# One-hot gate products of an expert layer: two 12-bit products in place of one fp32 product, and three of four plain masks made on ScalarE

## The chip, the cores and the metric

The kernel runs on one core of a Trainium2 chip. The metric is the time of one execution on the device in microseconds (us). Engines are named as the profile names them: PE is the matrix engine (PEld its loads of stationary operands), DVE the vector engine, ACT the scalar engine, POOL GpSimd, SP the queue that issues most transfers.

## The reference

The reference is a stack of three transformer layers on 256 tokens of width 1024. The change lies in the last part of the last layer, a layer of 16384 single-neuron experts of which every token uses 8 heads x 16:

```python
def peer(h, w_q, sub_keys, u_tab, v_tab):
    ...
    top_s, pos = lax.top_k(cand_s, PEER_TOPK)
    experts = jnp.take_along_axis(cand_i, pos, axis=-1)
    gates = jax.nn.softmax(top_s, axis=-1).astype(h.dtype)
    ...
    def one_chunk(args):
        hc, ec, gc = args
        u = u_tab[ec]
        a = jax.nn.gelu(jnp.einsum('td,thkd->thk', hc, u), approximate=False)
        return jnp.einsum('thk,thkd->td', gc * a, v_tab[ec])
```

An expert's number is 128 e + r with e (the block) and r (the row) from 0 to 127. `top_k` gives each token 128 (expert, gate) pairs.

## The kernel before, in words

The kernel does not gather experts. It computes gelu(h u) for all 16384 experts and all 256 tokens, multiplies it by a table W of gates that is zero where a token does not use an expert, and multiplies the result by all of v. This is `Peer.run`. Its first loop runs over b = 0..127, the blocks of 128 experts, in an order that is written out by hand: inside it ACT, DVE, POOL and PE each execute in the order in which the code names their instructions.

In one pass of that loop, `stream(b + 2)` loads a 512 KB block of u and splits it in a rounded part (`uhi`, ACT, L1235) and a rest (`ulo`, L1236, on POOL once the gates have begun); `first(b)` issues 24 products of 128x128 by 128x256 (L117 to L119); and `gelu` takes two finished blocks through ACT into W (L1258, L1261), with `times` (DVE, L1267) multiplying in the gates that are already there. `work` makes the gates' indices in between: DVE's top-16 searches up to about block 51, then `softmax` and `turn`, which lays experts' e, r and gates out by token in `col`.

From there on the gate table is built, five tokens with each pass (`RATE`). `masks_of` makes two 128x128 masks for a token on DVE: `a` (L1200) holds the gate where the place number equals e, `b` (L1201) holds one where it equals r. Both read the place numbers 0..127 from `places`, a copy of `iota` in a PSUM bank. `gates_of` multiplies them on PE (L1210) in fp32, which the trace records as two instructions for each product, and sums so the token's 128x128 gate table. `gates_out`, once for four tokens, copies the table's blocks that have no gelu yet to W on ACT (L1221) and multiplies the others into W on DVE (L1223). The masks lie in eight buffers in turn, and PE takes them four tokens late (`HOT`, `LAG`). The second loop, which multiplies W by v, is not touched.

Of the kernel before, what the change touches and what calls it, by code (L numbers as in the profile page):

```python
# [9 lines left out]
F32 = mybir.dt.float32  # L10
F32R = mybir.dt.float32r
# [3 lines left out]
AF = mybir.ActivationFunctionType  # L15
OP = mybir.AluOpType
# [6 lines left out]
S = 256  # L23
NT = 2
# [7 lines left out]
NCAND = sum((b - a) * w for a, b, w in RECT)  # L32
# [3 lines left out]
LEAD = 2  # L36
EARLY = 45
SPARE = 1.6
RATE = 5
HOT, LAG = 8, 4  # L40
PE = mybir.EngineType.PE
ORDERED = (mybir.EngineType.Activation, mybir.EngineType.DVE, mybir.EngineType.Pool, PE)
KEYS = ((1, 0), (0, 1), (2, 0), (3, 0), (1, 1), (2, 1), (3, 1))
# [40 lines left out]
class Net:  # L84
    def __init__(self, tc, ins, out, dbg):
        self.tc, self.nc, self.i, self.out, self.dbg = tc, tc.nc, ins, out, dbg
        self.bg = []
        self.n, self.pace, self.credit = 0, 1.2, 0.0
        self.normed = None
        self.mod, self.gate, self.loose = {}, {}, set()  # L90
# [1032 lines left out]
class Peer:  # L1123
# [3 lines left out]
    def __init__(self, net, s, pools):  # L1127
        self.net, self.s = net, s
        self.sp = sp = pools("route", 2)
        self.ef = [sp.tile([128, 128], F32, name=f"ef{t}", bufs=1) for t in range(NT)]  # L1130
        self.v = [sp.tile([128, 8, 16], F32, name=f"v{t}", bufs=1) for t in range(NT)]
        self.iota = sp.tile([128, 128], F32, name="iota", bufs=1)
        net.nc.gpsimd.dma_start(self.iota, net.i["k_iota"])
        self.line, self.full, self.count = [], [], 0
        self.parts = {}
        self.gated = self.active = 0

    def route(self, t, h):

        net, sp, s = self.net, self.sp, self.s  # L1140
        nc = net.nc
        one = sp.tile([128, 2, 16], F32, name="one")
        two = sp.tile([128, 2, 16], F32, name="two")
        both = sp.tile([128, 2, NCAND], F32, name="both")
        cs, ci = both[:, 0, :], both[:, 1, :]
        yield from top16(net, sp, s[t][:, 2 * h, :], 128, "t1", one[:, 0, :], one[:, 1, :], 128.0)
        yield from top16(net, sp, s[t][:, 2 * h + 1, :], 128, "t2", two[:, 0, :], two[:, 1, :], None)
        o = 0
        for a, b, wd in RECT:
            n = (b - a) * wd  # L1150
            nc.vector.tensor_tensor(both[:, :, o:o + n].rearrange("p m (a b) -> p m a b", b=wd),
                                    one[:, :, a:b, None].to_broadcast([128, 2, b - a, wd]),
                                    two[:, :, None, :wd].to_broadcast([128, 2, b - a, wd]), op=OP.add)
            o += n
        yield 0.8
        pos = sp.tile([128, 16], F32, name="pos")
        yield from top16(net, sp, cs, NCAND, "t3", self.v[t][:, h, :], pos, None)
        j = sp.tile([128, 16, NCAND], F32, name="ej", bufs=1)
        for k in range(16):
            nc.vector.scalar_tensor_tensor(j[:, k, :], self.iota[:, :NCAND], pos[:, k:k + 1], ci, op0=OP.is_equal,  # L1160
                                           op1=OP.mult, accum_out=self.ef[t][:, h * 16 + k:h * 16 + k + 1])
            if k % 4 == 3:
                yield 0.8
# [13 lines left out]
    def turn(self, t):  # L1177

        net, sp = self.net, self.sp
        nc = net.nc  # L1180
        x = sp.tile([128, 864], F32, name="ej", bufs=1)[:, :512].rearrange("p (a b) -> p a b", a=4)
        i0, i1 = x[:, 2, :].bitcast(I32), x[:, 3, :].bitcast(I32)
        nc.vector.tensor_copy(i0, self.ef[t])
        nc.vector.tensor_scalar(i1, i0, 7, None, op0=OP.arith_shift_right)
        nc.vector.tensor_copy(x[:, 0, :], i1)
        nc.vector.scalar_tensor_tensor(x[:, 1, :], x[:, 0, :], -128.0, self.ef[t], op0=OP.mult, op1=OP.add)
        p = net.wk()
        for k in range(2):
            nc.tensor.transpose(p[:, k * 128:(k + 1) * 128], x[:, k, :], net.ident)
        nc.tensor.transpose(p[:, 256:384], self.v[t].rearrange("p a b -> p (a b)"), net.ident)  # L1190
        nc.scalar.activation(self.col[:, t], p[:, :384].rearrange("p (k t) -> p k t", k=3), AF.Copy)

    def masks_of(self, n):

        nc = self.net.nc
        t, m = divmod(n, 128)
        a, b = (self.masks[:, self.count % HOT, j, :] for j in range(2))
        self.count += 1
        col = self.col[:, t]
        nc.vector.tensor_scalar(a, self.places, col[:, 0, m:m + 1], col[:, 2, m:m + 1], op0=OP.is_equal, op1=OP.mult)  # L1200
        nc.vector.tensor_scalar(b, self.places, col[:, 1, m:m + 1], None, op0=OP.is_equal)  # L1201
        self.line.append((n, a, b))

    def gates_of(self):

        n, a, b = self.line.pop(0)
        if n % 4 == 0:
            self.p = self.net.wk()
        k = n % 4
        self.net.nc.tensor.matmul(self.p[:, k * 128:(k + 1) * 128], b, a, start=True, stop=True)  # L1210
        if k == 3:
            self.full.append((n - 3, self.p))

    def gates_out(self):

# [67 lines left out]
    def run(self, W, h2T, spill):  # L1283

        net = self.net
        nc = net.nc
        self.W, self.h2T = W, h2T
        self.outs, self.late = [], []

        def work():  # L1290

            for n in range(1, 16):
                yield from self.route(n // 8, n % 8)
            cols = net.x8([128, 2048])
            self.col = cols[:, 0:768].rearrange("p (t k n) -> p t k n", t=NT, k=3)
            self.masks = net.x8([128, HOT, 2, 128])
            self.places = net.acc()[:, :128]
            nc.vector.tensor_copy(self.places, self.iota)
            self.tmp = [net.wk().rearrange("p (e t) -> p e t", e=2) for _ in range(2)]
            for t in range(NT):  # L1300
                self.softmax(t)
                yield 1.5
            for t in range(NT):
                self.turn(t)
                yield 1.0

        bg, credit, todo = work(), EARLY, list(range(S))
        for b in range(128):
            if b:
                credit += SPARE  # L1310
            while bg and credit > 0:
                cost = next(bg, None)
                if cost is None:
                    bg = None
                else:
                    credit -= cost
            if b + LEAD < 256:
                self.stream(b + LEAD, not bg and b + LEAD < 128)
            self.first(b)
            if not bg and todo is not None:  # L1320
                for _ in range(RATE):
                    if todo:
                        self.masks_of(todo.pop(0))
                    if len(self.line) > LAG or not todo:
                        if self.line:
                            self.gates_of()
                    if self.full:
                        self.gates_out()
                if not todo:
                    while self.line:  # L1330
                        self.gates_of()
                        if self.full:
                            self.gates_out()
                    todo = None
            self.times()
            if len(self.outs) > 1 or b == 127:
                while self.outs:
                    self.gelu()
                    if b < 127:
                        break  # L1340
        assert todo is None
        self.times()
        self.acc = {(t, c): net.acc() for t in range(NT) for c in range(2)}
        self.wx = net.x8([128, 4, 2, S], F32R)
        for e in range(2):
            self.weights(e)
        net.X = net.xp.tile([128, NT, D], F32, name="X")
        nc.gpsimd.dma_start(net.X, spill.rearrange("(t p) d -> p t d", p=128))
        for e in range(128):
            if e + LEAD < 128:  # L1350
                self.stream(128 + e + LEAD)
            if e + 2 < 128:
                self.weights(e + 2)
            self.second(e)
        for t in range(NT):
            for c in range(2):
                x = net.X[:, t, c * 512:(c + 1) * 512]
                nc.vector.tensor_tensor(x, x, self.acc[t, c], op=OP.add)
                (nc.scalar if c else nc.sync).dma_start(net.out[0, t * 128:(t + 1) * 128, c * 512:(c + 1) * 512], x)
# [259 lines left out]
```

## Time and profile before

| | us |
|---|---|
| median of three runs | 1845.95 (1845.42 to 1848.73) |
| the profiled execution | 1847.4, of which its span is 1845.6 |
| first loop, before the gate masks (1040.7 to 1195.3) | 154.6 |
| first loop, with gate masks (1195.3 to 1413.8) | 218.5 |
| first loop, after them (1413.8 to 1481.5) | 67.7 |

The span is the time from the first to the last instruction of the profiled execution; 1.8 us of that execution lie around it. The stages are stretches of the span, in us from its start. A single matrix product's duration includes the way through the array, so the pace of PE is read from the distance of starts or from counts over a stretch, not from durations.

### The profile page before, as it was taken

What the parts mean: (1) busy time and instruction counts of PE and PEld (TensorE: products, weight loads), DVE (VectorE), ACT (ScalarE), POOL (GpSimd) and SP (SyncE); (2) the same over time, 40 slices, a digit from 0 to 9 for tenths busy, and PEclk for the clock granted to TensorE, in tenths of its full rate; (3) what the DMA queues carried; (4) which work ended last, traced back from release to release, by engine and by line L of the source; (5) the groups of instructions that cost most, each with busy time, mean ns of one, the idle gap of its engine ahead of it and who ended that gap; (6) DMA issues with size and microseconds to landing.
All of it is one profiled execution on the core that took longest, in us unless ns stands there. A gap on an engine that the chain in (4) does not pass through costs nothing.

```text
span 1845.6 us, 28886 instructions
## 1 busy us (share of the span) xinstructions
PE 1772.3 (96%) x10804; PEld 1502.0 (81%) x10804; DVE 1296.4 (70%) x3228; ACT 862.5 (47%) x1258; POOL 218.9 (12%) x165
## 2 busy tenths in 40 slices
PE   7998999998999998998999999999999999999999
PEld 4764789887979997776885699999999978888887
DVE  3676788767876547785568899889997155555554
ACT  2444555544455435465543344544444444444443
POOL 2000000000000000000000000055556800000000
PEclk9999999998999999997999999999999999999999
DMA  9865379976757643553664166544444666666664
GB/s 356 253 209 170 115 247 317 311 254 216 260 173 253 195 150 115 182 169 96 193 233 144 60 185 184 168 130 125 135 118 143 186 207 191 185 190 186 189 187 149
DMA packets 144444, 347.38 MB, mean 188 GB/s; under 512 B 12469, under 2 KB 29901, under 8 KB 143152
## 3 DMA queue, kind: packets, MB, share of 16 engines
q1 hardware_dynamic: 139040, 331.93, 56.5%
q0 software_dynamic: 4688, 12.03, 2.0%
q8 instruction: 85, 1.39, 0.3%
q10 hardware_dynamic: 576, 1.57, 0.2%
q14 instruction: 55, 0.45, 0.1%
HBM read 343.36 MB, written 3.70 MB: 188 GB/s over the span
## 4 chain that ended last, share of the span: by engine, by line
PE 78%; DVE 15%; DMA 3%; ACT 3%; issue 1%; SPq 0%; DVEq 0%; ACTq 0%
PE acc L117 19%; PE acc L119 19%; PE acc L118 18%; PE wk L117 4%; PE wk L119 4%; PE wk L118 4%; DVE x L1200 2%; DVE ulo L1236 2%; PE wk L1210 2%; DVE x L1201 2%; PE acc L1072 2%; DVE W L1223 1%; DVE ej L1160 1%; DMA adaw<-in_ada_w 1%; PE wk L537 1%
## 5 line engine op out<-in xcount | busy, mean ns | idle before, releaser
L134 DVE TENSOR_TENSOR wlo<-raw,whi 128x1024 fp32r<-128x1024 f32 (+1 forms) x260 | 312.8, 1214 | 145.8 <-ACT whi L133 144.7
L1235 ACT ACTIVATE uhi<-raw 128x1024 fp32r<-128x1024 f32 x256 | 271.6, 1061 | 293.3 <-PE acc L119 177.8
L133 ACT ACTIVATE whi<-raw 128x1024 fp32r<-128x1024 f32 (+1 forms) x260 | 271.6, 1053 | 276.6 <-PE acc L119 96.7
L1236 DVE TENSOR_TENSOR ulo<-raw,uhi 128x1024 fp32r<-128x1024 f32 x182 | 222.5, 1223 | 174.3 <-ACT uhi L1235 173.9
L117 PE MATMUL acc<-x,uhi 128*128 128x256 f32 x1024 | 293.4, 287 | 0.0
L118 PE MATMUL acc<-X,uhi 128*128 128x256 f32 x1024 | 288.4, 282 | 0.0
L119 PE MATMUL acc<-x,ulo 128*128 128x256 f32 x1024 | 288.2, 281 | 0.0
L117 PE MATMUL acc<-whi,hT 128*128 128x512 f32 (+1 forms) x528 | 210.6, 400 | 9.4 <-ACT hT L138 7.6
L1236 POOL TENSOR_TENSOR ulo<-raw,uhi 128x1024 fp32r<-128x1024 f32 x74 | 177.0, 2393 | 352.5 <-ACT uhi L1235 352.4
L118 PE MATMUL acc<-wlo,hT 128*128 128x512 f32 (+1 forms) x528 | 207.3, 393 | 0.8 <-DVE wlo L134 0.7
L119 PE MATMUL acc<-whi,hT 128*128 128x512 f32 (+1 forms) x528 | 207.4, 393 | 0.3
L117 PE MATMUL acc<-uhi,x 128*128 128x512 f32 x512 | 202.3, 395 | 1.0 <-ACT x L138 1.0
L119 PE MATMUL acc<-uhi,x 128*128 128x512 f32 x512 | 202.3, 395 | 0.0
L118 PE MATMUL acc<-ulo,x 128*128 128x512 f32 x512 | 202.2, 395 | 0.0
L117 PEld LDWEIGHTS acc<-x,uhi 128*128 128x128 f32 x1024 | 193.9, 189 | 0.2 <-issue 0.2
L118 PEld LDWEIGHTS acc<-X,uhi 128*128 128x128 f32 x1024 | 193.8, 189 | 0.2 <-issue 0.2
L119 PEld LDWEIGHTS acc<-x,ulo 128*128 128x128 f32 x1024 | 193.7, 189 | 0.0
L117 PE MATMUL wk<-hT,whi 128*128 128x256 f32 x608 | 172.4, 284 | 0.0
L118 PE MATMUL wk<-hT,whi 128*128 128x256 f32 x608 | 171.9, 283 | 0.0
L119 PE MATMUL wk<-hT,wlo 128*128 128x256 f32 x608 | 171.8, 283 | 0.0
L117 PEld LDWEIGHTS acc<-whi,hT 128*128 128x128 f32 x528 | 101.1, 192 | 36.9 <-ACT hT L138 10.9
L119 PEld LDWEIGHTS acc<-whi,hT 128*128 128x128 f32 x528 | 101.0, 191 | 24.6 <-DVE hT L139 2.6
(371 smaller groups left out, 3057.4 us busy)
## 6 DMA issues: line engine op xcount, KB each, us to landing
raw<-in_mlp_w SPq DMA_DIRECT2D x128, 512.0 KB, 5.0
raw<-in_k_ut SPq DMA_DIRECT2D x128, 512.0 KB, 3.6
raw<-in_peer_v SPq DMA_DIRECT2D x128, 512.0 KB, 4.0
adaw<-in_ada_w SPq DMA_DIRECT2D x80, 512.0 KB, 5.0
raw<-in_w_in SPq DMA_DIRECT2D x52, 512.0 KB, 4.0
raw<-in_conv_w_in SPq DMA_DIRECT2D x24, 512.0 KB, 5.3
a<-in_k_a SPq DMA_DIRECT2D x8, 1024.0 KB, 8.2
raw<-in_attn_w_in SPq DMA_DIRECT2D x16, 512.0 KB, 8.2
```

The source lines that it names most:

```text
L117: nc.tensor.matmul(ps, ak(a[0]), bk(b[0]), start=start, stop=False, skip_group_check=True)
L118: nc.tensor.matmul(ps, ak(a[0]), bk(b[1]), start=False, stop=False, skip_group_check=True)
L119: self.last = nc.tensor.matmul(ps, ak(a[1]), bk(b[0]), start=False, stop=stop, skip_group_check=True)
L133: self.high = nc.scalar.activation(hi[:, :, :w], raw[:, :, :w], AF.Copy)
L134: self.low = nc.vector.tensor_tensor(lo[:, :, :w], raw[:, :, :w], hi[:, :, :w].bitcast(F32), op=OP.subtract)
L537: nc.tensor.transpose(p[:, k * 128:(k + 1) * 128], src[:, k * 128:(k + 1) * 128], net.ident)
L1072: nc.tensor.matmul(ps, self.hT[:, k, t * 128:(t + 1) * 128], self.slabs[c][k // 2][:, k % 2, j * n * 128:(j + 1) * n * 128], start=(k == 0 ...
L1200: nc.vector.tensor_scalar(a, self.places, col[:, 0, m:m + 1], col[:, 2, m:m + 1], op0=OP.is_equal, op1=OP.mult)
L1201: nc.vector.tensor_scalar(b, self.places, col[:, 1, m:m + 1], None, op0=OP.is_equal)
L1210: self.net.nc.tensor.matmul(self.p[:, k * 128:(k + 1) * 128], b, a, start=True, stop=True)
L1235: nc.scalar.activation(hi, raw, AF.Copy)
L1236: (nc.gpsimd if aside else nc.vector).tensor_tensor(lo, raw, hi.bitcast(F32), op=OP.subtract)
```

## The change

Each gate is cut in two parts that the reduced-precision type float32r (as which `uhi`, `ulo` and the activations already go to PE) holds exactly: a rounded gate (`col` row 3) and the rest (row 4). For each token DVE makes two `a` masks, one for each part, and PE sums two products, each one float32r product of 128x128 by 128x128. The plain masks `b` of three tokens of four are made on ACT: Square of (place - r), then one Relu(1 - square) over the three. The fourth `b` stays on DVE. `masks_of` and `gates_of` now take a group of four tokens, one group with each pass of the loop; the masks of a group lie in one of two halves of a buffer, and PE takes them one pass later. A pass first names the products of the group before, then the masks of its group, then `gates_out` of the group before.

```diff
-        self.col = cols[:, 0:768].rearrange("p (t k n) -> p t k n", t=NT, k=3)
-        self.masks = net.x8([128, HOT, 2, 128])
+        self.col = cols[:, 0:1536].rearrange("p (t k n) -> p t k n", t=NT, k=6)
+        self.one = cols[:, 1536:1537]
...
-        nc.scalar.activation(self.col[:, t], p[:, :384].rearrange("p (k t) -> p k t", k=3), AF.Copy)
+        col = self.col[:, t]
+        nc.scalar.activation(col[:, 0:3], p[:, :384].rearrange("p (k t) -> p k t", k=3), AF.Copy)
+        nc.scalar.activation(col[:, 3].bitcast(F32R), p[:, 256:384], AF.Copy)
+        nc.scalar.activation(col[:, 5], p[:, 128:256], AF.Copy, scale=-1.0)
+        nc.vector.tensor_tensor(col[:, 4], col[:, 2], col[:, 3], op=OP.subtract)
...
     def masks_of(self, n):
-        t, m = divmod(n, 128)
-        a, b = (self.masks[:, self.count % HOT, j, :] for j in range(2))
...
-        nc.vector.tensor_scalar(a, self.places, col[:, 0, m:m + 1], col[:, 2, m:m + 1], op0=OP.is_equal, op1=OP.mult)
-        nc.vector.tensor_scalar(b, self.places, col[:, 1, m:m + 1], None, op0=OP.is_equal)
+        t, g = n // 128, n // 4 % 2
+        a, b, col = self.hot[0][:, g], self.hot[1][:, g], self.col[:, t]
+        for k in range(4):
+            m = (n + k) % 128
+            for j in range(2):
+                nc.vector.tensor_scalar(a[:, k, j, :], self.places, col[:, 0, m:m + 1], col[:, 3 + j, m:m + 1],
+                                        op0=OP.is_equal, op1=OP.mult)
+            if k < 3:
+                nc.scalar.activation(b[:, k, :], self.places, AF.Square, bias=col[:, 5, m:m + 1])
+            else:
+                nc.vector.tensor_scalar(b[:, k, :], self.places, col[:, 1, m:m + 1], None, op0=OP.is_equal)
+        nc.scalar.activation(b[:, 0:3, :], b[:, 0:3, :].bitcast(F32), AF.Relu, scale=-1.0, bias=self.one)
         self.line.append((n, a, b))
...
-        self.net.nc.tensor.matmul(self.p[:, k * 128:(k + 1) * 128], b, a, start=True, stop=True)
+        for k in range(4):
+            for j in range(2):
+                self.net.nc.tensor.matmul(p[:, k * 128:(k + 1) * 128], b[:, k, :], a[:, k, j, :], start=(j == 0),
+                                          stop=(j == 1), skip_group_check=True)
...
-        bg, credit, todo = work(), EARLY, list(range(S))
+        bg, credit, todo = work(), EARLY, list(range(0, S, 4))
...
-                for _ in range(RATE):
-                    if todo:
-                        self.masks_of(todo.pop(0))
-                    if len(self.line) > LAG or not todo:
-                        if self.line:
-                            self.gates_of()
-                    if self.full:
-                        self.gates_out()
...
+                if self.line:
+                    self.gates_of()
+                if todo:
+                    self.masks_of(todo.pop(0))
+                if self.full:
+                    self.gates_out()
```

How the instructions stand on DVE before, early in the gate stage, between two of the multiplications into W (L1223); `acc` is the bank of `places`, the two `x` are the mask buffers and `col`; a wait in brackets names the engine whose counter is waited for:

```order
L1223 TENSOR_TENSOR W<-wk,W 128x4x52 [waits Activation_49]
L1200 TENSOR_SCALAR x_11836<-acc,x_11835 128x128 [waits DVE_49]
L1201 TENSOR_SCALAR x_11836<-acc,x_11835 128x128 [waits DVE_49]
L1200 TENSOR_SCALAR x_11836<-acc,x_11835 128x128 [waits DVE_49]
L1201 TENSOR_SCALAR x_11836<-acc,x_11835 128x128 [waits DVE_49]
```

And the same place of the changed kernel, between two of its multiplications (there L1232; L1203 is an `a` mask, L1209 the `b` mask that stays):

```order
L1232 TENSOR_TENSOR W<-wk,W 128x4x52 [waits Activation_49]
L1203 TENSOR_SCALAR x_11974<-acc,x_11835 128x128 [waits DVE_49] x2
L1203 TENSOR_SCALAR x_11974<-acc,x_11835 128x128 [waits Activation_49]
L1203 TENSOR_SCALAR x_11974<-acc,x_11835 128x128 [waits DVE_49]
L1203 TENSOR_SCALAR x_11974<-acc,x_11835 128x128 [waits Activation_49]
L1203 TENSOR_SCALAR x_11974<-acc,x_11835 128x128 [waits DVE_49]
L1203 TENSOR_SCALAR x_11974<-acc,x_11835 128x128 [waits Activation_49]
L1203 TENSOR_SCALAR x_11974<-acc,x_11835 128x128 [waits DVE_49]
L1209 TENSOR_SCALAR ej<-acc,x_11835 128x128 [waits DVE_49]
L1232 TENSOR_TENSOR W<-wk,W 128x4x54 [waits Activation_49]
L1276 TENSOR_TENSOR W<-W,wk 128x2x12
```

Before, no mask waits for ACT; now the first `a` mask of the second, third and fourth token does. By the counts of the program, each of these three waits is for the Square of the token just before it.

ACT before, in the same stretch, from one split of u (L1235) to the next:

```order
L1235 ACTIVATE uhi<-raw 128x1024 [waits DMAHW3_49,Pool_49]
L1221 ACTIVATE W<-wk 128x4x76 [waits PE_49] x2
L1258 ACTIVATE wk<-acc 128x2x16 [waits DVE_49]
L1261 ACTIVATE W<-acc 128x2x240
L1235 ACTIVATE uhi<-raw 128x1024 [waits DMAHW4_49,Pool_49]
```

ACT now (L1244 is the split of u, L1207 Square, L1210 Relu, L1230 the copy to W, L1267 and L1270 gelu):

```order
L1210 ACTIVATE ej<-ej,x_11835 128x384 [waits Activation_49]
L1230 ACTIVATE W<-wk 128x4x76 [waits PE_49]
L1267 ACTIVATE wk<-acc 128x2x12
L1270 ACTIVATE W<-acc 128x2x244
L1244 ACTIVATE uhi<-raw 128x1024 [waits DMAHW4_49,Pool_49]
L1207 ACTIVATE ej<-acc,x_11835 128x128 [waits DVE_49] x3
L1210 ACTIVATE ej<-ej,x_11835 128x384 [waits Activation_49]
L1230 ACTIVATE W<-wk 128x4x74 [waits PE_49]
```

Four more instructions stand between a split and the copy to W, and each Square waits for DVE: by the counts, for the second `a` mask of its own token. No table load stands between Square, Relu and Gelu. On PE, where five fp32 products stood behind a block's 24, eight products of the new kind stand now:

```order
L117 MATMUL acc<-x_9392,ulo 128x256
L1219 MATMUL wk<-x_11974,ej 128x128 [waits DVE_49,PE_49,Activation_49]
L1219 MATMUL wk<-x_11974,ej 128x128 [waits DVE_49] x6
L1219 MATMUL wk<-x_11974,ej 128x128
L115 MATMUL acc<-x_9392,uhi 128x256
```

The first of them waits for the Relu of its group, and the later ones for the group's DVE masks.

## Rows read from the trace of the kernel before

**Rows 1.** Busy time by engine, with gate masks and after: us, engines, PEclk, DMA share, GB/s.

```profile
1195.30:1413.80 218.50, 212.06 (x1779) 208.65 (x1779) 206.77 (x603) 97.09 (x169) 124.24 (x52) 1.00 0.42 127
1413.80:1481.50 67.70, 67.34 (x570) 67.14 (x568) 11.85 (x16) 31.59 (x38) 52.95 (x23) 1.00 0.60 184
```

**Rows 2.** The same stretches, L117 alone, eight instructions a block: PE, PEld.

```profile
1195.30:1413.80 218.50, 122.78 (x421) 79.47 (x422) 1.00 0.42 127
1413.80:1481.50 67.70, 53.12 (x190) 35.58 (x189) 1.00 0.60 184
```

**Rows 3.** Groups of instructions of the gate stage: xcount | busy us, mean ns | idle before.

```profile
L1200 DVE TENSOR_SCALAR x<-acc,x 128x128 f32<-128x128 f32 x256 | 105.6, 412 | 0.0
L1201 DVE TENSOR_SCALAR x<-acc,x 128x128 f32<-128x128 f32 x256 | 89.9, 351 | 0.0
L1210 PE MATMUL wk<-x 128*128 128x128 f32 x512 | 70.6, 278 | 6.4 <-DVE x L1201 3.5 <-ACT W L1221 2.7
L1223 DVE TENSOR_TENSOR W<-wk,W 128x224 f32<-128x224 f32 (+25 forms) x64 | 55.3, 863 | 11.7 <-ACT W L1221 11.2
L1221 ACT ACTIVATE W<-wk 128x288 f32<-128x288 f32 (+25 forms) x64 | 34.6, 541 | 118.8 <-PE wk L1210 118.8
L1267 DVE TENSOR_TENSOR W<-W,wk 128x512 f32<-128x512 f32 (+25 forms) x39 | 20.0, 512 | 47.8 <-ACT wk L1258 47.8
```

**Rows 4.** Timeline of DVE in the gate stage: start us, us, what.

```profile
1339.98 0.96 DVE L1223 TENSOR_TENSOR W<-wk,W 128x336 f32<-128x336 f32 x1
1340.84 0.40 DVE L1200 TENSOR_SCALAR x<-acc,x 128x128 f32<-128x128 f32 x1
1341.16 0.34 DVE L1201 TENSOR_SCALAR x<-acc,x 128x128 f32<-128x128 f32 x1
1341.42 0.40 DVE L1200 TENSOR_SCALAR x<-acc,x 128x128 f32<-128x128 f32 x1
```

**Rows 5.** Timeline of ACT in the gate stage, a gelu and the split behind it.

```profile
1344.49 0.56 ACT L1258 ACTIVATE wk<-acc 128x352 f32<-128x352 f32 x1
...
1345.16 1.06 ACT L1235 ACTIVATE uhi<-raw 128x1024 fp32r<-128x1024 f32 x1
```

**Rows 6.** Line 202 (min/median/max ns), and timelines of a transpose's read-out, ACT and DVE.

```profile
L202 ACT ACTIVATE hT<-wk,vec x8: 360/368/368, 958.9 to 985.9; 128x128 f32<-128x128 f32 x8
...
422.10 0.41 DVE L207 TENSOR_SCALAR full<-wk,af1A,af1B 128x128 f32<-128x128 f32 x1 [1.08 <-PE wk L193]
...
423.34 0.96 DVE L207 TENSOR_SCALAR full<-wk,af1A,af1B 128x128 f32<-128x128 f32 x2
...
422.55 0.46 ACT L202 ACTIVATE full<-wk,af1B,af1A 128x128 f32<-128x128 f32 x1 [0.29 <-DVE full L207]
423.40 0.46 ACT L202 ACTIVATE full<-wk,af1B,af1A 128x128 f32<-128x128 f32 x1 [0.40 <-DVE full L207]
```

**Rows 7.** Timeline of ACT in `turn`: 384 elements, and the next instruction.

```profile
1196.80 0.49 ACT L1191 ACTIVATE x<-wk 128x384 f32<-128x384 f32 x1 [1.36 <-PE wk L1190]
1197.19 1.05 ACT L1235 ACTIVATE uhi<-raw 128x1024 fp32r<-128x1024 f32 x1
```

**Rows 8.** Timelines of PE with idle before in brackets, windows of 1 us (PEclk third last).

```profile
167.63 0.66 PE L395 MATMUL wk<-ident,adab 128*128 128x128 f32 x4 [1.75 <-DVE adab L380]
...
168.00:169.00 1.00, 1.00 (x5) 0.36 (x5) 0.95 (x4) 0.00 (x0) 0.82 (x2) 0.72 0.68 275
...
974.80 0.44 PE L537 MATMUL wk<-ident,mr 128*128 128x128 f32 x2 [2.06 <-ACT mr L1076]
...
976.00:977.00 1.00, 1.00 (x7) 0.90 (x7) 0.90 (x8) 0.20 (x2) 0.00 (x0) 1.00 0.28 25
...
1193.38 0.41 PE L117 MATMUL acc<-x,uhi 128*128 128x256 f32 x1
1193.60 0.41 PE L118 MATMUL acc<-X,uhi 128*128 128x256 f32 x1
...
1195.91 0.29 PE L117 MATMUL acc<-x,uhi 128*128 128x256 f32 x1
```

More of the change, by code (lines that the diff above doesn't have):

```diff
@@ L38 @@
 SPARE = 1.6
-RATE = 5
-HOT, LAG = 8, 4
 PE = mybir.EngineType.PE
@@ L1133, in __init__ @@
         net.nc.gpsimd.dma_start(self.iota, net.i["k_iota"])
-        self.line, self.full, self.count = [], [], 0
+        self.line, self.full = [], []
         self.parts = {}
@@ L1157, in route @@
         yield from top16(net, sp, cs, NCAND, "t3", self.v[t][:, h, :], pos, None)
-        j = sp.tile([128, 16, NCAND], F32, name="ej", bufs=1)
+        j = sp.tile([128, 1024], F32, name="ej", bufs=1)[:, :16 * NCAND].rearrange("p (k n) -> p k n", k=16)
         for k in range(16):
@@ L1180, in turn @@
         nc = net.nc
-        x = sp.tile([128, 864], F32, name="ej", bufs=1)[:, :512].rearrange("p (a b) -> p a b", a=4)
+        x = sp.tile([128, 1024], F32, name="ej", bufs=1)[:, :512].rearrange("p (a b) -> p a b", a=4)
         i0, i1 = x[:, 2, :].bitcast(I32), x[:, 3, :].bitcast(I32)
@@ L1190, in turn @@
         nc.tensor.transpose(p[:, 256:384], self.v[t].rearrange("p a b -> p (a b)"), net.ident)
-        nc.scalar.activation(self.col[:, t], p[:, :384].rearrange("p (k t) -> p k t", k=3), AF.Copy)
+        col = self.col[:, t]
[3 more added lines that the diff above has]
+        nc.vector.tensor_tensor(col[:, 4], col[:, 2], col[:, 3], op=OP.subtract)
     def masks_of(self, n):
         nc = self.net.nc
-        t, m = divmod(n, 128)
-        a, b = (self.masks[:, self.count % HOT, j, :] for j in range(2))
-        self.count += 1
-        col = self.col[:, t]
-        nc.vector.tensor_scalar(a, self.places, col[:, 0, m:m + 1], col[:, 2, m:m + 1], op0=OP.is_equal, op1=OP.mult)
-        nc.vector.tensor_scalar(b, self.places, col[:, 1, m:m + 1], None, op0=OP.is_equal)
+        t, g = n // 128, n // 4 % 2
[10 more added lines that the diff above has]
+        nc.scalar.activation(b[:, 0:3, :], b[:, 0:3, :].bitcast(F32), AF.Relu, scale=-1.0, bias=self.one)
         self.line.append((n, a, b))
@@ L1206, in gates_of @@
         n, a, b = self.line.pop(0)
-        if n % 4 == 0:
-            self.p = self.net.wk()
-        k = n % 4
-        self.net.nc.tensor.matmul(self.p[:, k * 128:(k + 1) * 128], b, a, start=True, stop=True)
-        if k == 3:
-            self.full.append((n - 3, self.p))
+        p = self.net.wk()
+        for k in range(4):
+            for j in range(2):
+                self.net.nc.tensor.matmul(p[:, k * 128:(k + 1) * 128], b[:, k, :], a[:, k, j, :], start=(j == 0),
+                                          stop=(j == 1), skip_group_check=True)
+        self.full.append((n, p))
     def gates_out(self):
@@ L1294, in work @@
             cols = net.x8([128, 2048])
-            self.col = cols[:, 0:768].rearrange("p (t k n) -> p t k n", t=NT, k=3)
-            self.masks = net.x8([128, HOT, 2, 128])
+            self.col = cols[:, 0:1536].rearrange("p (t k n) -> p t k n", t=NT, k=6)
+            self.one = cols[:, 1536:1537]
+            nc.vector.memset(self.one, 1.0)
             self.places = net.acc()[:, :128]
@@ L1305, in work @@
                 yield 1.0
-        bg, credit, todo = work(), EARLY, list(range(S))
+            self.hot = (net.x8([128, 2, 4, 2, 128], F32R),
+                        self.sp.tile([128, 1024], F32R, name="ej", bufs=1).rearrange("p (g k n) -> p g k n", g=2, k=4))
+        bg, credit, todo = work(), EARLY, list(range(0, S, 4))
         for b in range(128):
@@ L1320, in run @@
             if not bg and todo is not None:
-                for _ in range(RATE):
-                    if todo:
-                        self.masks_of(todo.pop(0))
-                    if len(self.line) > LAG or not todo:
-                        if self.line:
-                            self.gates_of()
-                    if self.full:
-                        self.gates_out()
[L1329 to L1333, printed above, removed]
+                if self.line:
[4 more added lines that the diff above has]
+                    self.gates_out()
+                if not todo and not self.line:
                     todo = None
```

## The prediction

> **What bounds the kernel now.** I read the busy times by stretch first. While the gate table is built, DVE is busy 206.8 and PE 212.1 of 218.5 us; behind it PE is busy 67.3 of 67.7 [rows 1]. The reader is to see two engines at their limit side by side in the gate stage, and PE alone after it. Second, the same stretches for L117 alone, which stands eight times in a block [rows 2]: 421 instructions are 52.6 blocks with gates, 190 are 23.75 blocks without. So a block costs 67.7 / 23.75 = 2.85 us where PE sets the pace, and the gate stage 218.5 - 52.6 x 2.85 = 68.6 us more than its blocks alone. This 68.6 us is all that the change can win or must pay for. Third, the groups by line [rows 3] and DVE's timeline [rows 4]: a mask with a gate (L1200) holds DVE for 0.32 us from its start to the next one's, a plain mask (L1201) for 0.26; the multiplication into W (L1223, mean 0.86) is left 0.10 before it ends, so it holds DVE for 0.76. Fourth, the waits in the groups: DVE idles 0.0 before the masks, so before the change nothing stands between one mask and the next.
>
> **The change, part by part.**
>
> PE loses 512 recorded fp32 instructions. PE's busy time less the blocks is 212.1 - 149.9 = 62.2 us, 0.12 each. It gains eight float32r products of 128 columns for each group of four tokens. The trace has none. Below: half of a 256-column one, whose pace is 2.85 / 24 = 0.119, so 0.06. Above: as much as an fp32 product, 0.24. PE's block then takes 2.85 + 0.48 to 2.85 + 1.92, 3.3 to 4.8 us; I take the lower end, since one instruction passes where two did. It does not enter the sum if a block takes longer than 4.8 for other reasons, which is the case below.
>
> DVE's work for a group is eight `a` masks at 0.32, one `b` at 0.26, one multiplication into W at 0.76, and every second block the gelu's multiplication (mean 0.51, less the same 0.10, halved: 0.21): 3.79 us if nothing interrupts it. For 64 groups that is 64 x (3.79 - 2.85) = 60 us above the blocks, against 68.6 before. By busy time alone the change would win 8 us: for four tokens it adds four gate masks, at 0.32, and drops four plain ones but for one, at 0.26.
>
> But the masks are interrupted. The order of the changed kernel has DVE wait, at the second, third and fourth token, for ACT's Square of the token before, and each Square wait for DVE's two masks of its own token. Both read `places` in one PSUM bank. The trace of before shows the same pattern in the read-out of transposes, where DVE and ACT take turns on one bank [rows 6]: DVE ends at 422.10 + 0.41 = 422.51 and ACT starts at 422.55; ACT, started at 423.40, ends at 423.86, and the second DVE instruction of the pair from 423.34, 0.41 long, starts at 423.89. They never overlap on a bank; a handover costs 0.04 one way, 0.03 the other. The Trainium skill, page "PSUM — Partial Sum Buffer", section "PSUM bank collisions raise a hardware error", says that two engines must not access one bank in the same 32 partitions at once, reads against reads included, and that software has to keep them apart by bank; it speaks against placing ACT's masks here. By that rule the chain below is the sum, and by the view of busy times alone it would be the 8 us gain; the trace agrees with the rule.
>
> So I add up the chain of one block, from one copy to W on ACT to the next:
> - the copy, 0.54 (L1221's mean, [rows 3]), handover 0.03, DVE's multiplication 0.76, half a gelu multiplication 0.21, the first pair of masks 0.32 + 0.41 to its end = 0.73, handover 0.04: 2.31. ACT's own way in a block with gelu is 0.44 for the copy, 0.67 from a gelu to the split behind it, 0.96 for the split [rows 5], together 2.07: not later.
> - three Squares. The nearest row is an ACT instruction on 128x128 from PSUM with one pointer operand, 0.37 [rows 6]: 1.11. Between them two returns with a pair of masks, 0.03 + 0.73 + 0.04 each: 1.60.
> - then the Relu and the next copy, in order on ACT. 384 elements hold ACT 0.39 us [rows 7]; the pointer operand adds 0.46 - 0.37 = 0.09 [rows 6], its wait for the last Square 0.03: 0.51. DVE's last three masks take 0.03 + 0.32 + 0.32 + 0.34 = 1.01 in the same time, and the copy ends 0.51 + 0.54 behind the Square: they are hidden.
>
> Together 2.31 + 2.71 + 0.51 = 5.53 us for four tokens, above PE's 3.3 to 4.8. The 64 groups cost 64 x (5.53 - 2.85) = 171.5 us above the blocks in place of 68.6: **+103 us**. `turn` gains two ACT copies of 0.37 and a DVE subtraction of about 0.35 for each half of the tokens, ahead of the first masks: 0 to 2.2 us, I take 1. The sum is +104 us: 1847.4 + 104 = 1951.4 for a profiled execution, and 1846 + 104 = 1950 for the median, which lies 1.4 us below that execution.
>
> What is hidden and stays hidden: the split on POOL and the transfers, since blocks become longer; PE's products, unless they take over 2.7 us a block. What is late next is PE: it waits for masks 0.7 to 2.2 us in every block.
>
> Bounds. A pair of masks could end after 0.66 (0.32 + 0.34, as a plain mask does) or 0.82 (no overlap); a Square could take 0.46 like an instruction with two pointers; the Relu might pay no pointer; the six handovers might cost nothing, 0.2. A block then takes 5.03 to 6.07 us, the change costs 71 to 138, and the time lies at 1917 to 1984.
>
> **The rivals.**
> 1. *DVE alone sets the pace (faster).* If ACT's Squares cost DVE nothing, a block takes 3.79 us: 60 - 68.6 = -8 us, 1838. For it: busy times; the order of L1200 shows that DVE never waits today. Against it: the waits named in the order, which must be passed three times in a block. It decides if a block takes under 2.85 + 68.6 / 64 = 3.92 us. That needs the three Squares with their handovers, 1.3 us, and ACT's Relu and copy to vanish. Chance 0.04, and 0.01 that it lands within 0.2% of no change, which is about what a measurement can tell.
> 2. *PE falls to its lower clock.* With pauses of 0.7 to 2.2 us in every block PE may lose clock. A pause of 1.75 us at 167 was followed by a mean granted clock of 0.72, one of 2.06 at 975 by 1.00 [rows 8], so rows are of two minds. At 1.2 GHz products start 0.22 apart (1193.38, 1193.60), 24 take 5.3 us, and eight gate products twice 0.48 or more: 6.2 us a block or above, 64 x 3.35 - 68.6 = +146, 1992 and up. Against it: at that clock PE has no pauses left, and after 1193 the distance of durations was back at the fast level (0.29 at 1195.91). PE may also come late before ACT's copy feels it: the group's last mask ends some 0.5 us behind the copy's start, the products take up to 1.9, and the next copy is 5.5 away, which leaves 3 us. Chance that it holds for most of the stage: 0.09.
> 3. The forecast, waits between DVE and ACT with PE off the path: 0.86.
>
> **How the numbers follow.** The forecast is 1950. Its bounds give 1917 to 1984; I cut a little below, where three bounds must meet, and reach above into the second rival for clock falls in part of the stage: 1920 to 1990. Left out are most of rival 2, rival 1 and the forecast's edges, together just under 0.2. Faster by over 0.2%: 0.04; within: 0.01; slower: 0.95.
>
> **What the profile afterwards will show.** Right: DVE's masks idle for ACT's Square, three times a block, 0.4 us or more each; the Square idles for DVE's mask; splits of u start about 5.5 us apart in the stage, which lasts some 355 us for 64 blocks; PE's gate products wait for the last mask or the Relu; 11 blocks are left behind it in place of 24. Wrong: masks of DVE that start 0.32 apart across tokens (rival 1); products of u 0.22 apart through the stage (rival 2); a Square or Relu far from 0.37 and 0.5, which would change the size, not the sign.

## The result, and the profile after

The changed kernel takes 1953.19 us (median of four runs, 1950.52 to 1956.27) against 1845.68 us before (1845.17 to 1848.73): the ratio is 1.0579, with a 95% interval of 1.056 to 1.0599. The profiled execution took 1950.52 us, 103.1 us more than the one of before (1847.4).

The busy times and the granted clock on the page of the changed kernel (40 equal slices, in tenths):

```profile
PE   7998999989999989989999998788887899999999
...
DVE  3667787778775567855698997777777635555555
...
PEclk9999999989999999979999999988888899999999
```

The gate stage is about slices 25 to 32: there PE falls to seven or eight tenths and DVE to six or seven, where before they stood side by side near their limit [rows 1]. The stage by itself and the blocks left behind it (busy time of PE, PEld, DVE, ACT and POOL, granted clock, share of the DMA engines, GB/s):

```profile
1202.80:1549.00 346.20, 277.48 (x2025) 267.12 (x2024) 258.45 (x661) 206.17 (x443) 150.31 (x63) 0.92 0.32 98
1549.00:1582.00 33.00, 33.00 (x264) 33.00 (x264) 8.21 (x11) 15.38 (x19) 23.88 (x10) 0.95 0.55 166
```

The groups that answer to [rows 3] (L1203 is an `a` mask, L1207 the Square, L1210 the Relu, L1230 the copy to W, L1232 the multiplication into W, L1219 a gate product), over the gate stage:

```profile
L1203 DVE TENSOR_SCALAR x<-acc,x 128x128 fp32r<-128x128 f32 x509 | 185.2, 405 | 83.7 <-ACT ej L1207 83.7
...
L1219 PE MATMUL wk<-x,ej 128*128 128x128 f32 x512 | 72.3, 285 | 68.7 <-ACT ej L1210 68.5
L1207 ACT ACTIVATE ej<-acc,x 128x128 fp32r<-128x128 f32 x191 | 70.2, 367 | 139.6 <-DVE x L1203 138.9
...
L1232 DVE TENSOR_TENSOR W<-wk,W 128x200 f32<-128x200 f32 (+31 forms) x64 | 58.5, 914 | 5.3 <-ACT W L1230 3.9
L1210 ACT ACTIVATE ej<-ej,x 128x384 fp32r<-128x384 f32 x64 | 39.4, 615 | 2.1
L1230 ACT ACTIVATE W<-wk 128x312 f32<-128x312 f32 (+31 forms) x64 | 30.3, 473 | 0.0
```

The idle column is what to read. Before, it was 0.0 ahead of every mask; now DVE's masks stand 83.7 us for ACT's Square and the Squares stand 138.9 us for DVE's masks. The two wait for each other, and none of the 576 masks on DVE overlaps any of the 192 Squares in time. The chain of one block (start, length, what held it):

```profile
1402.09 0.94 DVE W L1232
1403.02 0.65 DVE x L1203 x2
1403.67 0.03 issue
1403.70 0.38 ACT ej L1207
1404.07 0.03 issue
1404.10 0.74 DVE x L1203 x2
1404.84 0.02 issue
...
1406.03 0.38 ACT ej L1207
1406.40 0.03 issue
1406.43 0.73 DVE x L1203 x2
1407.16 0.26 DVE ej L1209
...
1407.42 0.97 DVE W L1232
```

ACT's timeline behind the last of these Squares, Relu and copy to W:

```profile
1406.43 0.62 ACT L1210 ACTIVATE ej<-ej,x 128x384 fp32r<-128x384 f32 x1
1406.95 0.44 ACT L1230 ACTIVATE W<-wk 128x160 f32<-128x160 f32 x1
```

The copy reads the PSUM tile `wk` while DVE's last masks (1406.43 to 1407.42) read the bank of `places`, and neither waits for the other. So it is the one bank that is taken in turns, and not PSUM as such.

From 1402.09 to 1407.42 is 5.33 us for one group of four tokens. DVE's timeline gives the next group, which has a gelu multiplication, 1407.42 to 1413.15 = 5.73 (idle before an instruction, and what ended it, in brackets):

```profile
1407.42 0.97 DVE L1232 TENSOR_TENSOR W<-wk,W 128x352 f32<-128x352 f32 x1
1408.30 0.46 DVE L1276 TENSOR_TENSOR W<-W,wk 128x296 f32<-128x296 f32 x1
...
1409.84 0.73 DVE L1203 TENSOR_SCALAR x<-acc,x 128x128 fp32r<-128x128 f32 x2 [0.44 <-ACT ej L1207]
1411.01 0.73 DVE L1203 TENSOR_SCALAR x<-acc,x 128x128 fp32r<-128x128 f32 x2 [0.44 <-ACT ej L1207]
1412.17 0.73 DVE L1203 TENSOR_SCALAR x<-acc,x 128x128 fp32r<-128x128 f32 x2 [0.44 <-ACT ej L1207]
...
1413.15 0.97 DVE L1232 TENSOR_TENSOR W<-wk,W 128x352 f32<-128x352 f32 x1
```

Three waits of 0.44 us stand in each group; the mean of the two groups is 5.53 us.

### The profile page after: what moved, and what is told of

The parts are those of the page before. It is cut to its first block, busy times and chain, and to the rows that moved or that the text cites. A ratio compares the mean times of both kernels' runs of the same rounds, so it can differ in the third digit from the quotient of the medians.

```text
span 1948.7 us, 29223 instructions
## 1 busy us (share of the span) xinstructions
PE 1810.6 (93%) x10804; PEld 1533.3 (79%) x10804; DVE 1350.0 (69%) x3295; ACT 960.2 (49%) x1525; POOL 219.7 (11%) x165
## 4 chain that ended last, share of the span: by engine, by line
PE 68%; DVE 18%; ACT 8%; DMA 3%; issue 2%; SPq 0%; DVEq 0%; ACTq 0%
PE acc L115 17%; PE acc L117 17%; PE acc L116 16%; DVE x L1203 7%; PE wk L115 4%; PE wk L117 4%; PE wk L116 4%; ACT ej L1207 4%; DVE W L1232 2%; PE acc L1070 1%; ACT uhi L1244 1%; ACT W L1230 1%; DVE wlo L132 1%; DMA adaw<-in_ada_w 1%; PE wk L535 1%
## 5 line engine op out<-in xcount | busy, mean ns | idle before, releaser
L1244 ACT ACTIVATE uhi<-raw 128x1024 fp32r<-128x1024 f32 x256 | 271.2, 1060 | 277.7 <-PE acc L117 179.2
L115 PE MATMUL acc<-x,uhi 128*128 128x256 f32 x1024 | 305.1, 298 | 0.0
L117 PE MATMUL acc<-x,ulo 128*128 128x256 f32 x1024 | 300.7, 294 | 0.0
L116 PE MATMUL acc<-X,uhi 128*128 128x256 f32 x1024 | 299.5, 292 | 0.0
L1203 DVE TENSOR_SCALAR x<-acc,x 128x128 fp32r<-128x128 f32 x512 | 186.2, 405 | 84.2 <-ACT ej L1207 84.2
L117 PE MATMUL acc<-whi,hT 128*128 128x512 f32 (+1 forms) x528 | 207.0, 392 | 0.3
L116 PEld LDWEIGHTS acc<-X,uhi 128*128 128x128 f32 x1024 | 206.7, 202 | 0.2 <-issue 0.2
L115 PEld LDWEIGHTS acc<-x,uhi 128*128 128x128 f32 x1024 | 206.0, 201 | 0.2 <-issue 0.2
L117 PEld LDWEIGHTS acc<-x,ulo 128*128 128x128 f32 x1024 | 204.5, 200 | 0.0
L117 PE MATMUL acc<-uhi,x 128*128 128x512 f32 x512 | 203.1, 397 | 0.0
L117 PE MATMUL wk<-hT,wlo 128*128 128x256 f32 x608 | 171.8, 283 | 0.0
L1207 ACT ACTIVATE ej<-acc,x 128x128 fp32r<-128x128 f32 x192 | 70.5, 367 | 139.6 <-DVE x L1203 138.9
```

What stands on the lines that cost most here:

```text
L115: nc.tensor.matmul(ps, ak(a[0]), bk(b[0]), start=start, stop=False, skip_group_check=True)
L116: nc.tensor.matmul(ps, ak(a[0]), bk(b[1]), start=False, stop=False, skip_group_check=True)
L117: self.last = nc.tensor.matmul(ps, ak(a[1]), bk(b[0]), start=False, stop=stop, skip_group_check=True)
L1203: nc.vector.tensor_scalar(a[:, k, j, :], self.places, col[:, 0, m:m + 1], col[:, 3 + j, m:m + 1], op0=OP.is_equal, op1=OP.mult)
L1207: nc.scalar.activation(b[:, k, :], self.places, AF.Square, bias=col[:, 5, m:m + 1])
L1244: nc.scalar.activation(hi, raw, AF.Copy)
```

## The experiments

Two questions were open. Does the time come from the turns on the bank of `places`, or from something else in ACT's new work? And what would the change be worth without them? Eight kernels were run, most with one edit of the changed kernel. Each set of runs timed the kernel before again, and it took 1845.7 to 1848.9 us; so times of different sets compare to within some 3 us, and each ratio is to the kernel before of its own set.

**1. ACT's Squares read SBUF.** One operand: the Squares take the place numbers from `iota`, where `places` was copied from.

```diff
-                nc.scalar.activation(b[:, k, :], self.places, AF.Square, bias=col[:, 5, m:m + 1])
+                nc.scalar.activation(b[:, k, :], self.iota, AF.Square, bias=col[:, 5, m:m + 1])
```

> The changed kernel with one edit: ACT's Squares read the place numbers from iota in SBUF, so ACT and DVE no longer meet on the PSUM bank. Theory (turns on one bank): DVE's masks follow each other without a wait, a block takes DVE's own 3.8 us (8 x 0.32 + 0.26 + 0.82 + 0.19) to 4.0, so 1838 to 1851 us. Rival (ACT's added work and its place in the order are the cost, whatever it reads): no change, 1930 to 1960 us.

Measured: 1846.11 us, ratio to before 0.9986 (0.9973 to 1.0), 107.1 us less than the changed kernel. ACT's work is the same in number and no shorter (a Square takes 394 ns from SBUF, 367 from the bank), so the 107 us belong to the turns. The groups of its gate stage:

```profile
L1203 DVE TENSOR_SCALAR x<-acc,x 128x128 fp32r<-128x128 f32 x508 | 169.6, 436 | 0.0
...
L1207 ACT ACTIVATE ej<-iota,x 128x128 fp32r<-128x128 f32 x190 | 61.9, 394 | 0.0
```

L1207's and L1203's idle time is 0.0 again. And two of its windows show what sets the pace then: PE (first) alone at the start of the stage, later PE and DVE (third) together:

```profile
1220.00:1260.00 40.00, 40.00 (x343) 40.00 (x341) 38.20 (x112) 35.82 (x76) 24.75 (x11) 1.00 0.47 145
...
1340.00:1380.00 40.00, 40.00 (x342) 40.00 (x341) 40.00 (x108) 33.50 (x77) 24.50 (x11) 1.00 0.46 142
```

**2. The Squares behind all nine DVE masks.** The bank stays shared, but changes hands once each way in a block in place of three times.

```diff
-            if k < 3:
-                nc.scalar.activation(b[:, k, :], self.places, AF.Square, bias=col[:, 5, m:m + 1])
-            else:
-                nc.vector.tensor_scalar(b[:, k, :], self.places, col[:, 1, m:m + 1], None, op0=OP.is_equal)
+        nc.vector.tensor_scalar(b[:, 3, :], self.places, col[:, 1, m:m + 1], None, op0=OP.is_equal)
+        for k in range(3):
+            m = (n + k) % 128
+            nc.scalar.activation(b[:, k, :], self.places, AF.Square, bias=col[:, 5, m:m + 1])
```

> The changed kernel with the three Squares named after all nine DVE masks of a group, still on the PSUM bank: one turn from DVE to ACT and one back for each block in place of three. Theory (the chain of one block sets the pace): the masks 2.9, three Squares 0.93, Relu 0.52, copy 0.5 and DVE's multiplications 1.0 now stand one behind the other, 5.9 us a block, so about 1973 us, slower than the changed kernel. Rival (each turn has its price, some 0.43 us of DVE idling): two of three turns go, 64 x 2 x 0.43 = 55 us less, about 1898 us.

Measured: 1972.77 us, ratio 1.0661 (1.0638 to 1.0684). Fewer handovers, and slower. DVE's timeline:

```profile
1401.31 2.66 DVE L1203 TENSOR_SCALAR x<-acc,x 128x128 fp32r<-128x128 f32 x8
1403.86 0.36 DVE L1205 TENSOR_SCALAR ej<-acc,x 128x128 fp32r<-128x128 f32 x1
1406.18 0.94 DVE L1231 TENSOR_TENSOR W<-wk,W 128x336 f32<-128x336 f32 x1 [1.96 <-ACT W L1229]
```

ACT's in the same block, the three Squares, the Relu and the copy to W:

```profile
1404.26 0.88 ACT L1208 ACTIVATE ej<-acc,x 128x128 fp32r<-128x128 f32 x3 [3.29 <-DVE ej L1205]
1405.17 0.61 ACT L1209 ACTIVATE ej<-ej,x 128x384 fp32r<-128x384 f32 x1
1405.69 0.46 ACT L1229 ACTIVATE W<-wk 128x176 f32<-128x176 f32 x1
```

The masks run without a gap, but then Squares, Relu and copy follow in a row on ACT, and DVE stands 1.96 us in one piece where it stood 3 x 0.44 = 1.32. So the price is not one for each handover. It is the sum of what must run one after the other. In the changed kernel the last three DVE masks run beside Relu and copy; here nothing does.

**3. All masks on DVE.** Neither Square nor Relu; the two parts and the grouping stay.

```diff
-            if k < 3:
-                nc.scalar.activation(b[:, k, :], self.places, AF.Square, bias=col[:, 5, m:m + 1])
-            else:
-                nc.vector.tensor_scalar(b[:, k, :], self.places, col[:, 1, m:m + 1], None, op0=OP.is_equal)
-        nc.scalar.activation(b[:, 0:3, :], b[:, 0:3, :].bitcast(F32), AF.Relu, scale=-1.0, bias=self.one)
+            nc.vector.tensor_scalar(b[:, k, :], self.places, col[:, 1, m:m + 1], None, op0=OP.is_equal)
```

> The changed kernel with all four plain masks of a group on DVE and no Square or Relu. Theory: no turns, DVE's work sets the pace with 8 x 0.32 + 4 x 0.26 + 0.82 + 0.19 = 4.6 us a block, 64 x (4.6 - 2.85) - 68.6 = +44, about 1890 us. Rival (grouping by four with the products a pass later is itself the cost): 1930 us or above.

Measured: 1889.08 us, ratio 1.021 (1.0188 to 1.0233). DVE is busy 40.00 of 40 us in all windows of the stage. Against the first experiment, three masks of four on ACT are worth 43 us, as long as they don't read the bank that DVE reads; when they do, they cost some 64 us against leaving them on DVE (1953.2 - 1889.1, two sets of runs).

**4. The grouping alone.** Four tokens with each block, but one fp32 gate mask, one fp32 product, all masks on DVE, as before the change.

```diff
+        a, b = a.bitcast(F32), b.bitcast(F32)
...
-            for j in range(2):
-                nc.vector.tensor_scalar(a[:, k, j, :], self.places, col[:, 0, m:m + 1], col[:, 3 + j, m:m + 1],
-                                        op0=OP.is_equal, op1=OP.mult)
...
+            nc.vector.tensor_scalar(a[:, k, 0, :], self.places, col[:, 0, m:m + 1], col[:, 2, m:m + 1],
+                                    op0=OP.is_equal, op1=OP.mult)
+            nc.vector.tensor_scalar(b[:, k, :], self.places, col[:, 1, m:m + 1], None, op0=OP.is_equal)
...
+            self.net.nc.tensor.matmul(p[:, k * 128:(k + 1) * 128], b[:, k, :], a[:, k, 0, :], start=True, stop=True)
```

> The grouping alone: four tokens with each block as in the changed kernel, but one fp32 gate mask, one fp32 product and all masks on DVE, as before. Theory: PE sets the pace with 2.85 + 4 x 0.23 = 3.77 us a block against DVE's 3.3, so 3.8 to 3.9 us, 1838 to 1844 us, a little under the kernel before. Rival (the grouping costs by itself, since a group's products wait for the whole group before): 1855 us or above.

Measured: 1840.72 us, ratio 0.9958 (0.9942 to 0.9975). This part of the change, five tokens to four with each block and the new order of a pass, is a gain of 0.4%, and with it PE has no idle time left in the stage:

```profile
1202.00:1439.00 237.00, 237.00 (x2016) 237.00 (x2015) 210.69 (x590) 107.64 (x190) 149.12 (x63) 1.00 0.46 141
```

**5. One part only.** The first experiment without the second `a` mask and the second product of every token. It leaves out the rest of each gate, so the gates are rounded to the first part.

```diff
-            for j in range(2):
+            for j in range(1):
...
-            for j in range(2):
-                self.net.nc.tensor.matmul(p[:, k * 128:(k + 1) * 128], b[:, k, :], a[:, k, j, :], start=(j == 0),
-                                          stop=(j == 1), skip_group_check=True)
+            self.net.nc.tensor.matmul(p[:, k * 128:(k + 1) * 128], b[:, k, :], a[:, k, 0, :], start=True, stop=True)
```

> The kernel of the first experiment (Squares from SBUF) without the second gate mask and the second product, so the gates are rounded to 12 bits: that part of the computation is left out. It measures what a float32r product of 128 columns costs where PE alone sets the pace (DVE has 2.6 us of work a block). At 0.104, its distance in the profile after: 2.85 + 4 x 0.104 = 3.27 us a block, 64 x 0.42 - 68.6 = -42, about 1806 us. At 0.06, the lower bound of the prediction: 3.09, about 1794 us. If DVE's or ACT's work still set the pace: 1830 or above.

Measured: 1811.1 us, ratio 0.9803 (0.9788 to 0.9818). PE is busy in all of the stage (208.00 of 208), so its time is the price of the products. It speaks for the higher of the two prices.

**6. The fourth plain mask on ACT too.** The first experiment with four Squares and a Relu over 512 elements: DVE loses one mask of nine, ACT gains one.

```diff
-            if k < 3:
-                nc.scalar.activation(b[:, k, :], self.iota, AF.Square, bias=col[:, 5, m:m + 1])
-            else:
-                nc.vector.tensor_scalar(b[:, k, :], self.places, col[:, 1, m:m + 1], None, op0=OP.is_equal)
-        nc.scalar.activation(b[:, 0:3, :], b[:, 0:3, :].bitcast(F32), AF.Relu, scale=-1.0, bias=self.one)
+            nc.scalar.activation(b[:, k, :], self.iota, AF.Square, bias=col[:, 5, m:m + 1])
+        nc.scalar.activation(b, b.bitcast(F32), AF.Relu, scale=-1.0, bias=self.one)
```

> The first experiment, with the fourth plain mask on ACT too, all from SBUF. Theory (in the first experiment DVE, busy all the time, sets the pace at 3.75 us a block): DVE loses 0.26, then PE's 2.85 + 8 x 0.104 = 3.68 and DVE's 3.5 to 3.65 stand close together, 64 x (3.68 - 2.85) - 68.6 = -15, 1831 to 1838 us. Rival (ACT, with 3.5 to 3.7 us of work, becomes the bound or makes the copy to W late): 1840 to 1850 us.

Measured: 1841.94 us, ratio 0.9964 (0.995 to 0.9978): the time that the rival gave, but not for its reason. The stage:

```profile
1203.00:1440.00 237.00, 237.00 (x2020) 237.00 (x2019) 223.69 (x593) 222.79 (x503) 151.18 (x64) 1.00 0.48 142
```

ACT (fourth) and DVE (third) both have over 13 us to spare; PE has none. The stage lasts as long as in the fourth experiment, 237 us for 2020 and 2016 recorded instructions of PE. So two float32r products cost PE what one fp32 product does. By the difference to the fifth experiment, where PE is as full, a float32r product of 128 columns costs (1841.9 - 1811.1) / 256 = 0.12 us.

**7. DVE's masks read SBUF.** The mirror of the first experiment, meant to show that it does not matter who leaves the bank: the Squares stay on `places`, DVE's masks read `iota`.

```diff
-                nc.vector.tensor_scalar(a[:, k, j, :], self.places, col[:, 0, m:m + 1], col[:, 3 + j, m:m + 1],
+                nc.vector.tensor_scalar(a[:, k, j, :], self.iota, col[:, 0, m:m + 1], col[:, 3 + j, m:m + 1],
...
-                nc.vector.tensor_scalar(b[:, k, :], self.places, col[:, 1, m:m + 1], None, op0=OP.is_equal)
+                nc.vector.tensor_scalar(b[:, k, :], self.iota, col[:, 1, m:m + 1], None, op0=OP.is_equal)
```

> The changed kernel with the place numbers for DVE's masks taken from iota in SBUF, while ACT's Squares stay on the PSUM bank: the other way to keep the two off one bank. Theory (it is the shared bank): as the first experiment if a mask costs DVE the same from SBUF, 1838 to 1860 us. Rival (it is ACT's reading of PSUM beside its other work): 1930 us or above.

Measured: 1939.16 us, ratio 1.0497 (1.0474 to 1.052). By time alone the theory of the bank would have fallen. The groups say otherwise:

```profile
L1203 DVE TENSOR_SCALAR x<-iota,x 128x128 fp32r<-128x128 f32 x508 | 262.8, 586 | 0.0
...
L1207 ACT ACTIVATE ej<-acc,x 128x128 fp32r<-128x128 f32 x191 | 55.9, 372 | 0.0
```

No one waits for the bank any more: the idle time is 0.0 on both sides. Instead the masks themselves have become long, 586 ns in the mean against 405. The single masks of L1203, of the whole execution and of two that start around 1405 (shortest, median and longest in ns, first and last start):

```profile
L1203 DVE TENSOR_SCALAR x<-iota,x x512: 327/335/2558, 1198.7 to 1537.3; 128x128 fp32r<-128x128 f32 x171
...
L1203 DVE TENSOR_SCALAR x<-iota,x x2: 339/1408/2478, 1405.0 to 1405.3; 128x128 fp32r<-128x128 f32 x2
```

And the timelines of POOL and DVE in that block:

```profile
1405.16 2.54 POOL L1245 TENSOR_TENSOR ulo<-raw,uhi 128x1024 fp32r<-128x1024 f32 x1 [2.45 <-ACT uhi L1244]
...
1404.02 4.27 DVE L1203 TENSOR_SCALAR x<-iota,x 128x128 fp32r<-128x128 f32 x8
1408.22 0.27 DVE L1209 TENSOR_SCALAR ej<-iota,x 128x128 fp32r<-128x128 f32 x1
```

The median mask takes 335 ns, and one in this block takes 2478: it starts at 1405.3, just behind the start of POOL's split of u at 1405.16, and ends when that has ended (1407.70). The whole stage is like it: 65 masks take over 0.5 us, each lies beside one of POOL's splits and ends 0.08 to 0.09 us behind the end of one, and of the 66 splits only the last, at 1539.6, has no such mask. The new theory: a DVE mask with its input in SBUF stands still while POOL's split runs.

**8. That, with POOL's split on DVE.** No POOL instruction is left to stand still for; DVE gets some 65 splits more in the stage.

```diff
-        (nc.gpsimd if aside else nc.vector).tensor_tensor(lo, raw, hi.bitcast(F32), op=OP.subtract)
+        nc.vector.tensor_tensor(lo, raw, hi.bitcast(F32), op=OP.subtract)
```

> DVE's masks from SBUF as in the kernel with these alone (1939.2 us), and the second part of every stream split on DVE; none on POOL. Theory (a mask that reads SBUF stands still while POOL's split runs): in that kernel's trace eight masks take 4.27 us in a block with one POOL split of 2.5 us; undisturbed masks start 0.265 us apart, so the standstill is 4.2 - 8 x 0.265 = 2.1 us a block. It goes, and a split of 1.15 us on DVE comes: 64 x (1.15 - 2.1) = -61 us, so about 1878 us (1865 to 1890), no mask over 0.4 us. Rival (a mask that reads SBUF is at times slow by itself, or from DMA or TensorE's reads): masks keep their mean of 0.585 us and the split comes on top, 64 x 1.15 = +74 us: about 2010 us.

Measured: 1873.18 us, ratio 1.0138 (1.011 to 1.0166). DVE has more to do and the kernel is 66 us faster than the seventh. DVE's timeline in a block:

```profile
1341.13 1.33 DVE L1245 TENSOR_TENSOR ulo<-raw,uhi 128x1024 fp32r<-128x1024 f32 x1
1342.27 2.25 DVE L1203 TENSOR_SCALAR x<-iota,x 128x128 fp32r<-128x128 f32 x8
1344.32 0.40 DVE L1209 TENSOR_SCALAR ej<-iota,x 128x128 fp32r<-128x128 f32 x1
```

Eight masks pass in 2.05 us from start to start, 0.26 each, where they took 4.2 with POOL at work (1404.02 to 1408.22 above). One detail of the expectation failed: the recorded length of a mask grows through the stage, to a median of 1.09 us for the last 61, although eight of them still start within 2.05 us (1440.94 to 1442.99). It isn't the input in SBUF: in the third experiment, where the masks read PSUM and DVE is busy all the time too, the records of L1203 reach 1.46 us, while each starts at most 0.32 before the next instruction. So here the distance of starts is to be read, not the durations; why the records grow stays open. By that distance the standstill is gone: at most 0.26 us from a mask of L1203 to the next instruction in this stage, up to 2.48 in the seventh experiment.

## Why the prediction was right, point by point

- *Turns on one bank.* They are there as forecast: three waits of DVE in each group, 191 in all for 83.7 us, 0.44 each (forecast at least 0.4), and handovers of 0.02 to 0.03 (forecast 0.03 and 0.04, [rows 6]). The first experiment shows that the shared bank is the whole of the loss: take ACT off it, and 107 us go. The rule of the Trainium skill that the prediction weighed, page "PSUM — Partial Sum Buffer", section "PSUM bank collisions raise a hardware error", fits the rows of this kernel: none of the 576 DVE masks lies beside a Square on that bank. The waits that see to it stand in the program; what the chip would do without them, no run shows.
- *The chain of one block.* Its three pieces, in the group at 1402 without a gelu multiplication: from the multiplication into W to the first Square 1.61 us (forecast 0.76 + 0.73 + 0.04 = 1.53), three Squares with two returns 1403.70 to 1406.40 = 2.70 (2.71), from there to the next multiplication 1.02 (0.51 + 0.54 + 0.03 = 1.08). Together 5.33 against 5.32, and with the gelu multiplication 5.73 against 5.74. That the sum fits to 0.01 is luck in part: the multiplication into W holds DVE for 0.85 (1402.09 to the first mask at 1402.94) where the forecast had 0.76, and the last piece is 0.06 shorter than forecast.
- *Its last piece* was right by a hair's breadth only. I had ACT's Relu and copy end it. In the chain above DVE's own masks do (1407.42, the copy at 1407.39), since the copy is shorter than I took (0.47 in the mean, for 0.54); ACT's copy is what the multiplication waits for in 18 groups of 64, for 3.9 us in all. The Relu holds ACT for 0.52 (1406.43 to 1406.95, forecast 0.51).
- *The sum.* The stage lasts 346.2 us from its first to its last gate product, which are 63 blocks apart: 5.50 each (forecast 5.53, some 355 for 64). 11 blocks are left (264 products, 24 each), and the profiled execution is 1950.5 us against 1951.4. Two small misses about cancel in it: 64 blocks at 5.50 are 2 us less than forecast, and the 11 blocks behind them take 3.00 us each in place of 2.85, 1.7 us more.
- *PE's products* were mis-sized, at no cost. I took the lower bound of 0.06 us. Eight of them, with the last one 0.275 long, take 1.05 us, so they start (1.05 - 0.275) / 7 = 0.11 apart, just under half of what an fp32 product takes. PE had to wait for ACT's Relu all the same, 68.5 us in all, though 47 times in 64 groups and not in every block as forecast; but this price decides the kernels without turns (experiments 1 and 6).
- *PE's lower clock* (the second rival) came in part of the stage, and the time did not follow. PE's timeline in one block:

```profile
1401.76 1.24 PE L1219 MATMUL wk<-x,ej 128*128 128x128 f32 x8 [1.67 <-ACT ej L1210]
...
1403.55 0.41 PE L115 MATMUL acc<-x,uhi 128*128 128x256 f32 x1
1403.76 0.41 PE L116 MATMUL acc<-X,uhi 128*128 128x256 f32 x1
...
1407.15 1.05 PE L1219 MATMUL wk<-x,ej 128*128 128x128 f32 x8
```

  Two windows of the same block (granted clock third last):

```profile
1403.00:1405.50 2.50, 2.50 (x14) 2.50 (x14) 1.63 (x6) 1.30 (x3) 1.85 (x1) 0.50 0.00 0
1406.50:1409.00 2.50, 2.50 (x23) 2.50 (x23) 2.49 (x7) 1.75 (x3) 0.68 (x1) 1.00 0.63 202
```

  Behind a pause of 1.67 us the granted clock is 0.50 (1.2 GHz), and products start 0.21 apart; later in the same block it is 1.00. PE then takes its gate products at 1407.15 with no wait for masks, and the multiplication that needs them (1413.15 in DVE's timeline) doesn't wait either: PE had that much room. In the whole stage the clock was 0.92, and a block took 5.50 us, not the 6.2 of this rival.
- *The first rival* (DVE alone sets the pace, 1838) is the first experiment, and that gives 1846. DVE's own sum, 60 us above the blocks, was near enough; but PE, at 0.11 to 0.12 us for each of 512 products, comes to 56 to 61 us and is as long.

So where did the gain go? Piece by piece: four tokens with each block in place of five, in the new order, gives 0.4% (the fourth experiment against before); the second mask and product of each token then cost 48 us (the third against the fourth; DVE is full there); ACT gives 43 of it back from SBUF (the first against the third), and the shared bank takes 107. Even without that, two float32r products cost PE as much as the one fp32 product that they replace, so the best kernel with two parts (1841.9 us) is no better than the grouping alone (1840.7). These two are the fastest full kernels of the study, and their intervals overlap.

## What to carry to other kernels

Before a second engine takes over part of a job, look at which memory bank its operand lies in. Here the first engine read that bank in the same loop, the two took turns, and what looked like relief became one chain of both. Reading the operand elsewhere removed that, but see who works there too: the same move was free for ACT, and for DVE it cost nearly all that it won (1939 us against 1953). And when an expected gain is lost, find out what it would have been without the loss; here PE's price for the products left almost nothing to win.

## What the runs showed of the hardware beyond that

- A DVE mask with a gate starts 0.26 us before the next instruction when it reads SBUF, 0.32 when it reads PSUM ([rows 4] and the chain above). But with its input in SBUF one mask in a block stands still until POOL is through its 128x1024 elements (2.5 us); with its input in PSUM none does: in the stage of the first experiment the longest of 508 takes 533 ns and each starts at most 0.32 us before the next instruction, with POOL busy 24.5 of 40 us:

```profile
L1203 DVE TENSOR_SCALAR x<-acc,x x508: 389/433/533, 1199.8 to 1445.0; 128x128 fp32r<-128x128 f32 x170
```

  The Trainium skill, page "SBUF — State Buffer", section "SBUF: two separate sides", tells of a pair of ports that DVE, in some of its instructions, and GpSimd lock against each other for a whole instruction. The seventh and eighth experiments agree with it.
- POOL hardly suffers from this: its split takes 2.42 us in the mean there, 2.39 where the masks read PSUM.
- A float32r product of 128 columns costs PE 0.11 to 0.12 us (0.11 by its starts in the changed kernel, 0.12 by the fifth and sixth experiments), hardly less than one of 256 columns (2.85 / 24 = 0.119). Halving the columns gave next to nothing here.
